# Expert matrices in runs of 8 KB: another order of the contraction rows in the expert layers of a two-layer hybrid model

## Chip, cores and metric

The kernel runs on one core of one Trainium2 chip. The metric is the device time of one execution in microseconds (us). Three runs of the kernel before are known: 1325.94, 1326.06 and 1327.15 us, with a median of 1326.06 us. The profiled execution took 1326.32 us; its instructions span 1324.5 us.

## The reference

Each of the two layers has a mixer (retention and RWKV-7), a cross-attention to a memory, and a mixture of experts; every one is followed by a layer norm. The change concerns the experts alone:

```python
# t: 256 tokens x 1024; 16 experts; combine[t, e] is nonzero for 2 experts of each token
for e in range(16):
    h = silu(t @ w_gate[e]) * (t @ w_up[e])      # w_gate, w_up: [1024, 512]
    y = y + combine[:, e:e+1] * (h @ w_down[e])  # w_down: [512, 1024]
```

All of it is float32. In both products a sum over the rows of a matrix (1024 or 512 of them) is taken, and the order of the rows in that sum is free.

## The kernel before

Weights come from HBM in pieces of 1 MB, all issued by SyncE (SP, line L150 in `fetch`). `piece` (L184) says which part of a matrix a piece is: with `(k p) c -> p k c` partition p gets the rows p, 128 + p, 256 + p and so on, so a partition's share of a piece lies in several separate places in HBM. A gate or up matrix is two pieces, each of four rows of 2 KB per partition; a down matrix is two pieces, each of two rows of 4 KB per partition. One layer's experts are 16 x 3 x 2 = 96 pieces. They go into a ring of buffers (tiles `raw`, `wh`, `x` and `A`; L1122 adds the last three for the expert stage). SP issues a piece as soon as its buffer has been read for the last time, so pieces are fetched far ahead of use.

`moe` (L1099) runs one layer of experts. L1107 to L1115 turn x around with TensorE and split it into two float32r parts (`rx`); `route` (L1021) computes from these which tokens go to which expert, in a long chain of small VectorE operations that begins with `big` (L1036). Beside it, L1117 to L1119 split x as it is, without turning it, into `xs[0]` and `xs[1]`: ScalarE copies x into the first (L135), and VectorE subtracts (L136) to get the rest. L1124 to L1127 put x itself into the accumulators `py` with eight multiplications by a unit matrix `identr`, of 512 columns each. `gather` (L1184), once for four experts, multiplies slices of 128 columns of `xs` by a one-hot matrix `oh`; out come the tokens of the four experts, already turned, as four tiles `xe`, each with two blocks of 128 model columns. The block index k there must mean the same model columns as the index k of the weight pieces.

L1132 to L1166 go over pairs of experts p. `expert_in` (L1231) does one gate or up product: two pieces, four multiplications each; the token block (`xe`, 64 columns) is stationary in TensorE and the weights stream through. Two multiplications for the upper and the lower half of the output rows lie side by side in the array; `halves` (L1242) adds the two halves with a ScalarE copy to `low` (L1246) and a VectorE addition (L1247). `expert_mid` (L1249) turns the activations of a pair, [128 tokens, 512], with four transposes of 128 columns each (`tr`, L131: the slice of the activation is loaded into TensorE as weights, and the unit matrix streams through); VectorE copies the result to `hT` (L1255). `expert_out` (L1258) is the down product. The PE rows of these products are `g<-raw,xe` and `g<-raw,hT` (or `wh`, `x`, `A` for `raw`), of the transposes `g<-cst,act`, of the unit-matrix products `y<-xs,identr`, of the gather `g<-oh,xs`. In these names the streamed operand stands before the loaded one. An instruction of the program in float32 can show as two rows: four multiplications of `expert_in` are eight matmuls in the trace.

A layer ends with `norm` (L269), the prefetch of two pieces for the next layer (L1173), a branch `tc.If(n > 0)` that all engines pass (L1175), and the layer norm. The body of the branch, `overflow` (L1289), is for an expert with more than 64 tokens. No instruction of it is in the trace. After the first layer's branch `memory` (L942) loads the memory `mem` again in four parts into `sg` (L951), turns them and starts the next layer's products.

Program order is not the order of an engine: a scheduler lays out each engine's instructions by their dependences when the program is built. One line of `moe` (L1139) forces an order, that the first expert's products stand behind the first one-hot.

Of the kernel before, what the change touches and what calls it, by code (L numbers as in the profile page):

```python
# [9 lines left out]
F32 = mybir.dt.float32  # L10
# [10 lines left out]
D = 1024  # L21
DK = D // 128
# [3 lines left out]
FE = 512  # L26
# [78 lines left out]
def flat(ap):  # L105

    n = len(ap.shape) - 1
    names = " ".join("abcdefg"[:n])
    return ap.rearrange(f"p {names} -> p ({names})") if n > 1 else ap
# [6 lines left out]
class Build:  # L116
# [66 lines left out]
    @staticmethod  # L183
    def piece(w, k0, nk, c0, n):  # L184
        return w.rearrange("(k p) c -> p k c", p=128)[:, k0:k0 + nk, c0:c0 + n], [128, nk, n]

    @staticmethod
    def finish(steps):
# [910 lines left out]
    def moe(self, l, x, mem):  # L1099
        tc, nc, a, c = self.tc, self.nc, self.a, self.c  # L1100
        wg, wu, wd = a["moe_w_gate"][l], a["moe_w_up"][l], a["moe_w_down"][l]
        py = [[self.pp.tile([128, 512], F32, name="y", tag="a", bufs=2) for _ in range(2)]]
        with ExitStack() as ctx:
            mo = ctx.enter_context(tc.tile_pool(name="moe", bufs=1))
            with tc.tile_pool(name="route", bufs=1) as rp:
                rx = []
                for k in range(0, DK, 2):  # L1107
                    ps = self.pp.tile([128, 2, 2, 128], F32, name="g", tag="b", bufs=4)
                    for j in range(2):
                        for tb in range(2):  # L1110
                            self.tr(ps[:, j, tb, :], x[:, tb, (k + j) * 128:(k + j + 1) * 128])
                    if k % 4 == 0:
                        t = self.wpool.tile([128, 2, 2, 2, 256], F32R, name="rx", tag="wh", bufs=self.nhi)
                    rx.append([t[:, k // 2 % 2, i] for i in range(2)])
                    self.split(flat(ps), flat(rx[-1][0]), flat(rx[-1][1]))  # L1115
                rank, cws, cover, flag = self.route(rx, rp, mo, self.small)
            xs = [self.xt.tile([128, 2, D], F32R, name=f"xs{i}", tag=f"xT{i}") for i in range(2)]  # L1117
            for tb in range(2):
                self.split(x[:, tb, :], xs[0][:, tb, :], xs[1][:, tb, :])  # L1119
            if l + 1 < self.layers:  # L1120
                self.spill_values(l + 1, mem, 0)
            self.ring = self.ring + [(self.wpool, "wh", self.nhi)] * self.nhi + [(self.xp, "x", 1)] + ([(self.aux, "A", 2)] * 2 if l + 1 < self.layers else [])  # L1122
            py.append([self.pp.tile([128, 512], F32, name="y", tag="c", bufs=2) for _ in range(2)])
            for tb in range(2):  # L1124
                for jc in range(2):
                    for i in range(2):
                        self.mm(py[tb][jc], self.identr, xs[i][:, tb, jc * 512:jc * 512 + 512], i == 0, False)  # L1127
            lists, acts, ys = {}, {}, {}
            step = self.gather(mo, 0, xs, rank, cws, lists)
            self.finish(step)  # L1130

            for p in range(NP + 2):  # L1132
                if p < NP:
                    if p % 2 == 0 and p < NP - 2:
                        step = self.gather(mo, p // 2 + 1, xs, rank, cws, lists)
                    xe = lists[p // 2][0]
                    act = mo.tile([128, 512], F32, name="act", bufs=2)
                    for o in range(2):
                        with self.behind(self.onehot) if p == 0 and o == 0 and NM > 0 else ExitStack():  # L1139
                            ps = self.expert_in(wg[2 * p + o], [t[:, :, 2 * (p % 2) + o] for t in xe])  # L1140
                        self.halves(mo, ps, act, o)
                        next(step, None)
                    nc.scalar.activation(act, act, AF.Silu)
                    acts[p] = act
                if 1 <= p <= NP:
                    hT = self.expert_mid(mo, acts.pop(p - 1))
                if p < NP:
                    if p >= 2:
                        self.combine(p - 2, ys.pop(p - 2), lists[(p - 2) // 2][1][:, p % 2], py)
                    us = self.aux.tile([128, 512], F32, name="us", tag="sg", bufs=3)  # L1150
                    for o in range(2):
                        ps = self.expert_in(wu[2 * p + o], [t[:, :, 2 * (p % 2) + o] for t in xe])
                        self.halves(mo, ps, us, o)
                        next(step, None)
                    nc.vector.tensor_mul(out=act, in0=act, in1=us)
                    if p % 2:
                        self.finish(step)
                if 1 <= p <= NP:
                    y = [self.aux.tile([128, 512], F32, name="y", tag="sg", bufs=3) for _ in range(2)]
                    for o in range(2):  # L1160
                        self.expert_out(mo, wd[2 * p - 2 + o], hT, y, o)
                        if p == NP and o == 0:
                            self.combine(p - 2, ys.pop(p - 2), lists[(p - 2) // 2][1][:, p % 2], py)
                    ys[p - 1] = self.weighed(mo, y, lists[(p - 1) // 2][2][:, (p - 1) % 2:(p - 1) % 2 + 1])
                if p == NP + 1:
                    self.combine(p - 2, ys.pop(p - 2), lists[(p - 2) // 2][1][:, p % 2], py)  # L1166
        self.extra.close()
        self.ring = [r for r in self.ring if r[1] == "raw2"]
        gb = self.norm(a["ln3_g"][l], a["ln3_b"][l])
        self.ring = [(self.wpool, "raw", self.nraw)] * self.nraw  # L1170
        if l + 1 < self.layers:
            w = a["xa_wkv"][l + 1]
            self.prefetch([self.piece(w, hf * 4, 4, D + 512, 512) for hf in range(2)])  # L1173
        n = nc.values_load(flag[0:1, 0:1], min_val=0, max_val=2 * S)
        with tc.If(n > 0):  # L1175
            self.overflow(l, xs, py, cover)
        x = self.xp.tile([128, 2, D], F32, name="x")

        self.layer_norm(lambda tb, j: py[tb][j], gb, x, LN_EPS / ALPHA ** 2)
        self.tail.close()  # L1180
        self.tap("ln3", x)
        return x
# [48 lines left out]
    def expert_in(self, w, xe):  # L1231

        ps = self.pp.tile([128, 512], F32, name="g", tag="b", bufs=4)
        for hf in range(2):
            raw = self.take(*self.piece(w, hf * 4, 4, 0, FE))
            for k in range(0, 4, 2):
                t = xe[hf * 2 + k // 2]
                for j in range(2):
                    self.mm(ps[j * 64:j * 64 + 64, :], t[:, j], raw[:, k + j, :], hf == 0 and k == 0, hf == 1 and k == 2)
        return ps  # L1240
# [8 lines left out]
    def expert_mid(self, mo, g):  # L1249

        ps = self.pp.tile([128, 4, 128], F32, name="g", tag="b", bufs=4)
        for f in range(4):
            self.tr(ps[:, f, :], g[:, f * 128:f * 128 + 128])
        hT = mo.tile([128, 4, 128], F32, name="hT", bufs=1)
        self.nc.vector.tensor_copy(out=flat(hT), in_=flat(ps))  # L1255
        return hT

    def expert_out(self, mo, wd, hT, y, o):  # L1258

        pd = [self.pp.tile([128, 512], F32, name="g", tag="b", bufs=4) for _ in range(2)]  # L1260
        for hf in range(2):
            raw = self.take(*self.piece(wd, hf * 2, 2, 0, D))
            for jc in range(2):
                for j in range(2):
                    self.mm(pd[jc][j * 64:j * 64 + 64, :], hT[:, hf * 2 + j, o * 64:o * 64 + 64], raw[:, j, jc * 512:jc * 512 + 512], hf == 0, hf == 1)
        for jc in range(2):
            self.halves(mo, pd[jc], y[jc], o)
# [21 lines left out]
    def overflow(self, l, xs, py, cover):  # L1289

        tc, nc, a = self.tc, self.nc, self.a
        pp = self.pp
        with tc.tile_pool(name="ov", bufs=1) as op:
            x = op.tile([128, 2, D], F32, name="ox")
            nc.vector.tensor_add(out=flat(x), in0=flat(xs[0]).bitcast(F32), in1=flat(xs[1]).bitcast(F32))
            xT = op.tile([128, DK, 256], F32, name="oxT")
            for k in range(0, DK, 2):
                ps = pp.tile([128, 2, 2, 128], F32, name="otp", tag="b", bufs=4)
# [4 lines left out]
            with tc.For_i(0, NE, 1) as e:  # L1303
                wd = op.tile([128, 4, D], F32, name="owd")
# [4 lines left out]
                for fh in range(2):  # L1309
                    w = []  # L1310
# [54 lines left out]
```

## Time and profile before

| | |
|---|---|
| runs | 1325.94, 1326.06, 1327.15 us |
| profiled execution | 1326.32 us, its span 1324.5 us |
| TensorE busy (PE) | 1225.4 us, 93% of the span |
| TensorE weight loads (PEld) | 856.1 us, beside PE |
| VectorE (DVE) | 759.1 us, 57% |
| ScalarE (ACT) | 494.9 us, 37% |
| GpSimd (POOL) | 73.0 us, 6% |
| DMA | 331.10 MB, mean 250 GB/s |

A line of the profile names line, engine, operation, what is written and what is read, the shape, and the count; behind the bar stand the busy time, the mean time of one in ns, and the idle time of the engine before it with what ended that. The timeline gives start, duration and the same names, equal neighbours merged. The expert stage of the first layer lies between 463 and 685 us, that of the second between 1085 and 1312 us.

### The profile page before, as it was taken

The page shows a single profiled execution, that of the slowest core. Times are in us where ns is not written, and L with a number is a line of the kernel's source. Part 1 is how long each engine was busy: PE and PEld are TensorE (multiplying, and loading weights), DVE is VectorE, ACT ScalarE, POOL GpSimd, SP SyncE. Part 2 cuts the span into 40 slices and gives each one's busy share as a digit, 9 for nine tenths or more (in the row PEclk, how much of TensorE's full clock was granted, in tenths as well). Part 3 has the DMA queues.
Part 4 walks back from the last instruction along what each step waited for, and adds up shares of the span by engine and source line. Part 5 has one row for each costly group of instructions (what it writes and reads, how often), then busy time and mean ns, then how long its engine had stood idle before and what let it go on. Part 6 is the DMA issues. An engine that isn't in the chain of part 4 may idle for free. (4 is left out here: it accounts for less than half of the span.)

```text
span 1324.5 us, 20023 instructions
## 1 busy us (share of the span) xinstructions
PE 1225.4 (93%) x7952; PEld 856.1 (65%) x7952; DVE 759.1 (57%) x1518; ACT 494.9 (37%) x785; POOL 73.0 (6%) x125
## 2 busy tenths in 40 slices
PE   7998998998999999999969998989979969999995
PEld 7886687796888844333329976877959854434331
DVE  6588677487557523333366787865775562333335
ACT  4556333253544322322235663332534312232222
POOL 0012221000000000000000103210000000000000
PEclk9999989999999999999989999999999979999997
DMA  9745132198834899999997452231888349999994
GB/s 318 263 148 180 50 97 76 33 323 290 276 127 175 304 398 402 398 397 402 399 341 228 159 179 72 85 96 48 302 291 312 120 166 349 402 396 401 401 396 194
DMA packets 189843, 331.10 MB, mean 250 GB/s; under 512 B 23152, under 2 KB 80880, under 8 KB 188720
## 3 DMA queue, kind: packets, MB, share of 16 engines
q1 hardware_dynamic: 187728, 324.51, 68.2%
q10 hardware_dynamic: 1728, 3.15, 0.7%
q0 software_dynamic: 288, 2.10, 0.4%
q8 instruction: 66, 1.08, 0.3%
q14 instruction: 33, 0.27, 0.1%
HBM read 321.86 MB, written 7.87 MB: 249 GB/s over the span
## 5 line engine op out<-in xcount | busy, mean ns | idle before, releaser
L136 DVE TENSOR_TENSOR wh<-raw,wh 128x1024 fp32r<-128x1024 f32 (+1 forms) x204 | 232.7, 1143 | 111.0 <-ACT wh L135 109.5
L135 ACT CAST wh<-raw 128x1024 fp32r<-128x1024 f32 (+1 forms) x204 | 199.8, 981 | 155.0 <-PE acc L127 138.5
L127 PE MATMUL acc<-xT,wh 128*128 128x256 f32 x1824 | 247.7, 289 | 2.7 <-DVE xT L136 1.6
L127 PEld LDWEIGHTS acc<-xT,wh 128*128 128x128 f32 x1824 | 225.9, 190 | 11.2 <-DVE xT L136 1.9
L1246 ACT COPY low<-g 64x512 f32<-64x512 f32 x128 | 74.2, 580 | 289.4 <-PE g L127 263.5
L127 PE MATMUL g<-raw,xe 128*64 128x512 f32 x688 | 157.7, 598 | 4.5 <-DVE hT L1255 3.4
L127 PE MATMUL acc<-wh,xT 128*128 128x512 f32 x384 | 101.9, 408 | 3.0 <-DVE vg L557 3.0
L127 PEld LDWEIGHTS g<-raw,xe 128*64 128x64 f32 x688 | 46.0, 136 | 90.7 <-issue 79.9
L1247 DVE TENSOR_TENSOR y<-g,low 64x512 f32<-64x512 f32 x64 | 44.1, 689 | 77.0 <-ACT low L1246 75.8
L127 PE MATMUL g<-raw,hT 128*64 128x512 f32 x352 | 81.4, 596 | 5.2 <-DVE hT L1255 2.6
L127 PEld LDWEIGHTS acc<-wh,xT 128*128 128x128 f32 x384 | 70.1, 188 | 21.5 <-DVE vg L557 3.8
L1247 DVE TENSOR_TENSOR us<-g,low 64x512 f32<-64x512 f32 x32 | 22.0, 689 | 94.4 <-ACT low L1246 94.3
L1247 DVE TENSOR_TENSOR act<-g,low 64x512 f32<-64x512 f32 x32 | 22.0, 689 | 75.2 <-ACT low L1246 75.1
L127 PEld LDWEIGHTS g<-raw,hT 128*64 128x64 f32 x352 | 26.1, 137 | 54.6 <-issue 41.7
L127 PE MATMUL acc<-wh,memT 128*128 128x512 f32 x192 | 51.0, 417 | 0.0
L127 PE MATMUL acc<-memT,wh 128*128 128x256 f32 x384 | 46.5, 282 | 1.6 <-DVE wh L136 1.2
L127 PEld LDWEIGHTS acc<-memT,wh 128*128 128x128 f32 x384 | 45.7, 188 | 2.6 <-DVE wh L136 1.7
L127 PE MATMUL acc<-wh,oT 128*128 128x512 f32 x192 | 45.6, 394 | 1.0 <-DVE x L406 0.8
L127 PE MATMUL acc<-wh,mT 128*128 128x512 f32 x192 | 45.7, 397 | 0.7 <-DVE xr L406 0.7
L127 PE MATMUL acc<-ys,wh 128*128 128x256 f32 x384 | 45.1, 279 | 0.0
L127 PEld LDWEIGHTS acc<-ys,wh 128*128 128x128 f32 x384 | 45.0, 188 | 0.0
L127 PEld LDWEIGHTS g<-oh,xs 128*128 128x128 f32 x256 | 33.4, 196 | 17.1 <-issue 11.2
(310 smaller groups left out, 1700.6 us busy)
## 6 DMA issues: line engine op xcount, KB each, us to landing
raw<-in_w_in_dram SPq DMA_DIRECT2D x46, 1024.0 KB, 5.1
raw<-in_moe_w_down_dram SPq DMA_DIRECT2D x44, 1024.0 KB, 14.9
raw<-in_moe_w_gate_dram SPq DMA_DIRECT2D x43, 1024.0 KB, 13.9
raw<-in_moe_w_up_dram SPq DMA_DIRECT2D x43, 1024.0 KB, 13.8
raw<-in_xa_wkv_dram SPq DMA_DIRECT2D x16, 1024.0 KB, 10.2
wh<-in_moe_w_up_dram SPq DMA_DIRECT2D x15, 1024.0 KB, 14.2
A<-in_moe_w_down_dram SPq DMA_DIRECT2D x10, 1024.0 KB, 13.6
A<-in_moe_w_gate_dram SPq DMA_DIRECT2D x9, 1024.0 KB, 13.7
```

The lines of the kernel that those rows point to most:

```text
L127: self.nc.tensor.matmul(out, lhsT, rhs, start=start, stop=stop, skip_group_check=True)
L135: self.nc.scalar.copy(out=hi, in_=src)
L136: (eng or self.nc.vector).tensor_sub(out=lo, in0=src, in1=hi)
L1246: self.nc.scalar.copy(out=low[h], in_=ps[x])
L1247: self.nc.vector.tensor_add(out=out[h], in0=ps[h], in1=low[h])
```

## The change

The rows of the expert matrices are dealt to the partitions in another way: with `(p k) c -> p k c` partition p gets neighbouring rows, 8p to 8p + 7 of a gate or up matrix and 4p to 4p + 3 of a down matrix. A piece, half of these rows, is then one run of 8 KB in HBM per partition. Three things follow. `xs` is written with its columns in the matching order: the split reads x in steps of eight elements and writes neighbouring places, so that the slices that `gather` takes stay as they were. The products with the unit matrix must put x back into its own order, so their streamed operand is read across `xs` in steps of 128 elements. And the transposes of `expert_mid` take each fourth column of the activation. `overflow` gets two additions in the other order for its one.

```diff
+    def together(w, hf):
+        n = w.shape[0] // 128
+        return w.rearrange("(p k) c -> p k c", k=n)[:, hf * (n // 2):hf * (n // 2) + n // 2, :], [128, n // 2, w.shape[1]]
...
             for tb in range(2):
-                self.split(x[:, tb, :], xs[0][:, tb, :], xs[1][:, tb, :])
+                self.split(*(t[:, tb, :].rearrange(r, k=DK) for t, r in ((x, "q (p k) -> q k p"), (xs[0], "q (k p) -> q k p"), (xs[1], "q (k p) -> q k p"))))
...
-                        self.mm(py[tb][jc], self.identr, xs[i][:, tb, jc * 512:jc * 512 + 512], i == 0, False)
+                        self.mm(py[tb][jc], self.identr, xs[i][:, tb, :].rearrange("q (k p) -> q p k", k=DK)[:, jc * 64:jc * 64 + 64, :], i == 0, False)
...
-            raw = self.take(*self.piece(w, hf * 4, 4, 0, FE))
+            raw = self.take(*self.together(w, hf))
...
-            self.tr(ps[:, f, :], g[:, f * 128:f * 128 + 128])
+            self.tr(ps[:, f, :], g[:, f:FE:4])
...
-            raw = self.take(*self.piece(wd, hf * 2, 2, 0, D))
+            raw = self.take(*self.together(wd, hf))
```

## Rows read from the trace of the kernel before

**Rows 1.** The head of the page: span, and busy time of the engines.

```profile
span 1324.5 us, 20023 instructions
PE 1225.4 (93%) x7952; PEld 856.1 (65%) x7952; DVE 759.1 (57%) x1518; ACT 494.9 (37%) x785; POOL 73.0 (6%) x125
```

**Rows 2.** Stretches of 20 us, second layer: busy by engine, PEclk, DMA share, GB/s; sum.

```profile
1120.00:1140.00 20.00, 19.79 (x94) 7.15 (x96) 8.54 (x13) 7.31 (x12) 0.00 (x0) 1.00 1.04 398
...
sum 80.00, PE 77.94 PEld 29.08 DVE 33.02 ACT 26.19 POOL 0.00; mean PE 19.48 PEld 7.27 DVE 8.26 ACT 6.55 POOL 0.00
```

**Rows 3.** Waits in 470 to 685 us: total us, times, longest us.

```profile
PE g L127 <- DVE hT L1255: 3.4, 4, 1.3
...
PE g L127 <- DVE y L1247: 2.5, 5, 0.5
...
PE g L127 <- DMA raw<-in_moe_w_down_dram: 0.4, 1, 0.4
```

**Rows 4.** First layer, timeline of SP and PE: an early and a late piece.

```profile
501.23 4.71 SPq L150 DMA_DIRECT2D A<-in_moe_w_gate_dram  x1
...
539.88 1.51 PE L127 MATMUL g<-A,xe 128*64 128x512 f32 x6
...
649.40 11.82 SPq L150 DMA_DIRECT2D raw<-in_moe_w_down_dram  x6
...
664.23 1.94 PE L127 MATMUL g<-raw,hT 128*64 128x512 f32 x8 [0.38 <-DMA raw<-in_moe_w_down_dram]
```

**Rows 5.** DMA issues at 501.2 and 649.4 us, issue to landing in us.

```profile
A<-in_moe_w_gate_dram SPq DMA_DIRECT2D x1, 1024.0 KB, 16.0
...
raw<-in_moe_w_down_dram SPq DMA_DIRECT2D x1, 1024.0 KB, 14.7
```

**Rows 6.** DMA packets in 541 to 553 us, in 657 to 675 us; a transfer in 8 KB rows.

```profile
DMA packets 2323, 4.63 MB, mean 386 GB/s; under 512 B 67, under 2 KB 67, under 8 KB 2322
...
DMA packets 1932, 7.45 MB, mean 414 GB/s; under 512 B 116, under 2 KB 116, under 8 KB 1931
...
kT<-keys SPq DMA_DIRECT2D x2, 1024.0 KB, 4.8
```

**Rows 7.** Groups on DVE, shapes apart: L812 reads in steps of 16 elements, L814 doesn't.

```profile
L812 DVE TENSOR_TENSOR blkT<-blkO,blkM 64x225 f32<-64x225 f32 x4 | 2.1, 535 | 0.1
...
L814 DVE TENSOR_REDUCE blkO<-blkT 64x15 f32<-64x225 f32 x4 | 1.5, 379 | 0.1
...
L812 DVE TENSOR_TENSOR blkT<-blkO,blkM 64x1 f32<-64x1 f32 x4 | 0.6, 147 | 1.5 <-DMA blkM<-blkin 1.5
```

**Rows 8.** The split of x for the gather, shapes apart; second layer's timeline, DVE.

```profile
L136 DVE TENSOR_TENSOR xs<-x,xs 128x1024 fp32r<-128x1024 f32 x4 | 4.9, 1218 | 0.5 <-ACT xs L135 0.5
...
L135 ACT CAST xs<-x 128x1024 fp32r<-128x1024 f32 x4 | 4.2, 1046 | 15.4 <-DVE x L301 15.4
...
1072.26 2.48 DVE L136 TENSOR_TENSOR rx<-g,rx 128x512 fp32r<-128x512 f32 x4
```

**Rows 9.** PE timeline: unit-matrix products, first layer, then second layer up to the router.

```profile
441.98 0.87 PE L127 MATMUL y<-xs,identr 128*128 128x512 f32 x3
442.69 1.09 PE L127 MATMUL g<-rx,rw 128*32 128x256 f32 x8
...
1072.30 2.06 PE L127 MATMUL y<-xs,identr 128*128 128x512 f32 x4
1074.15 1.53 PE L127 MATMUL g<-rx,rw 128*32 128x256 f32 x9
...
1076.44 0.52 PE L127 MATMUL g<-rx,rw 128*32 128x256 f32 x3
```

**Rows 10.** Transposes of the activation: all weight loads as a group; one set, timeline.

```profile
L131 PEld LDWEIGHTS g<-cst,act 128*128 128x128 f32 x64 | 7.0, 141 | 8.4 <-issue 7.3 <-DVE y L1247 0.8
...
1230.30 0.42 PEld L131 LDWEIGHTS g<-cst,act 128*128 128x128 f32 x4 [0.81 <-issue]
```

**Rows 11.** The chain that ended last, 680 to 700 us: start, us, what.

```profile
684.68 2.74 DMA sg<-in_mem_dram
```

More of the change, by code (lines that the diff above doesn't have):

```diff
@@ L185, in piece @@
         return w.rearrange("(k p) c -> p k c", p=128)[:, k0:k0 + nk, c0:c0 + n], [128, nk, n]
+    @staticmethod
+    def together(w, hf):
+        n = w.shape[0] // 128
+        return w.rearrange("(p k) c -> p k c", k=n)[:, hf * (n // 2):hf * (n // 2) + n // 2, :], [128, n // 2, w.shape[1]]
     @staticmethod
@@ L1294, in overflow @@
             x = op.tile([128, 2, D], F32, name="ox")
-            nc.vector.tensor_add(out=flat(x), in0=flat(xs[0]).bitcast(F32), in1=flat(xs[1]).bitcast(F32))
+            for tb in range(2):
+                nc.vector.tensor_add(out=x[:, tb, :].rearrange("q (p k) -> q k p", k=DK), in0=xs[0][:, tb, :].bitcast(F32).rearrange("q (k p) -> q k p", k=DK),
+                                     in1=xs[1][:, tb, :].bitcast(F32).rearrange("q (k p) -> q k p", k=DK))
             xT = op.tile([128, DK, 256], F32, name="oxT")
```

## The prediction

> **What bounds the kernel now.** I began at the head of the page: TensorE is busy in 93% of the span, so time is won or lost mostly there [rows 1]. In the expert stage the windows show two resources that are full at once: in four stretches of 20 us PE is busy for 19.48 us of each on the mean at full clock, and the DMA engines move about 400 GB/s with a share at 1 [rows 2]. Shares don't say which of the two ends last, so I went on to the waits: in the first layer's expert stage PE waited 3.4 us for `hT`, 2.5 us for the additions of L1247, and 0.4 us for a weight piece [rows 3]. Then to single pieces. One is issued at 501.23 us, lands 16.0 us later, at 517.2 us, and is first used at 539.88 us: it lies ready for 22.6 us. A late one, issued at 649.40 us, lands 14.7 us later, at 664.1 us, and its product starts at 664.23 us, after a wait of 0.38 us [rows 4, 5]. So TensorE sets the pace nearly to the end of the stage; the DMA falls behind it, uses up the lead of 22.6 us, and the two meet in the last pieces only. What speeds up transfers can win the little that is waited for there; what lengthens TensorE's work counts in full.
>
> **The transfers.** Nothing is added to or taken from SP's or POOL's queue: 192 pieces of 1 MB stay 192, in the same order. The packets are fewer. A stretch with rows of 2 KB alone moved 386 GB/s, one with rows of 4 KB alone 414 GB/s [rows 6]: 1,048,576 bytes take 2.72 and 2.53 us. Per piece that is 512 and 256 packets over 16 engines, 32 and 16 on each, so 16 packets cost 0.18 us, or 11.4 ns each. With 8 KB there are 8 on each engine, and my estimate is 2.53 - 8 x 0.0114 = 2.44 us. An expert has four pieces of the first kind and two of the second: 15.94 us now, 14.64 us then, and 20.8 us less of transfers for a layer's 16 experts. The other bound: a whole transfer in 8 KB rows landed in 4.8 us and is not seen to beat the 4 KB rows [rows 6]; at their price the saving is 12 us. I take the first, since the two rates are long stretches and the other is one short transfer; it matters little, because these microseconds lie beside TensorE's work. On the path I count the wait of 0.4 us and, after the branch, the load of the memory: its first part takes 2.74 us on the chain [rows 11] right behind the last weights, and might come 0.4 us sooner. Together -0.8 us, with 0 and -1.5 us as bounds. What is late next when the pieces are early: the same waits for `hT` and L1247 as now.
>
> **The price of a long step.** Three edits read SBUF in steps of 8, 128 and 4 elements, where neighbours were read. Nearest in the trace is L812, whose first operand goes in steps of 16 elements: 225 elements take 535 ns and one takes 147 ns, so 1.73 ns for each. L814 has the same number of elements in the same number of rows, without a step: (379 - 147) / 224 = 1.04 ns [rows 7]. The long step costs 0.69 ns per element, in this row of VectorE. No row shows TensorE or ScalarE with one; for them it is bounded by nothing on one side and by one element per 1.73 ns on the other. A gain is excluded: the same elements are read, only farther apart. I take 1.73 ns for all three, as it is the only row there is and all three read the same memory.
>
> [...]
>
> **The split of x.** VectorE's share grows by 1024 x 0.69 = 0.7 us on top of 1.22 us, ScalarE's copy, with that price, by 0.7 us on top of 1.05 us [rows 8]; twice per layer. In the first layer both stand beside products of the memory that TensorE has in stock, so they cost nothing; without that cover it would be 1.4 us. In the second layer the first of them stands ahead of the four splits `rx` at 1072.26 us [rows 8], for which the router waits: 1.4 us later, in the chain with the next edit.
>
> **The unit-matrix products.** In the first layer three of them start 0.71 us before the next product, 0.24 us each [rows 9]. 512 elements at 1.73 ns are 0.89 us: 0.65 us more each. In the first layer eight stand in a gapless row of PE work: +5.2 us. In the second, four stand ahead of the router's products at 1072.30 us, two more between them, and two behind [rows 9]. There the rest of the first split is ready at about 1073.7 instead of 1072.3 us; two products that read it take until 1075.5 us, then come the router's products and two more of these, which now end at 1076.96 us, 2.81 us after 1074.15. After: 1075.5 + 2.81 + 2 x 0.65 = 1079.6 us, so +2.7 us with the split in it. The last two run while VectorE routes, at no cost. Bounds for both layers: 1.4 us (the split alone) and 7.9 us; I take 7.9.
>
> **The transposes.** 64 loads of 128 columns take 141 ns each now, and four of a set take 0.42 us [rows 10]. At 1.73 ns a column a load is 221 ns, so +0.08 us each, +0.32 us a set, +5.1 us for the 16 sets, since PE is full there. Bounds: 0, if the loads vanish beneath products before them, and 64 x (0.221 - 0.105) = 7.4 us, if nothing overlaps. I take 5.1. Behind a set wait VectorE's copy to `hT` and the down product.
>
> [...]
>
> **The rest.** `overflow` is not entered; its two additions cost nothing. The one-hot, the gather's products and the copies keep their shapes and steps.
>
> **Sum.** 1326.3 - 0.8 + 5.2 + 2.7 + 5.1 = 1338.5 us against the profiled execution, which stands 0.3 us above the median; 1338 us in terms of the median. With all upper bounds: 1326.3 + 7.9 + 7.4 = 1341.6 us.
>
> **Rivals.** (1) TensorE doesn't feel the step: then ScalarE and VectorE alone pay, 1.4 us in the second layer, against -0.8 us: 1327 us, no change. For it: its streams and loads have rows without steps only, and those take 0.24 us for 512 columns [rows 9], far quicker per element than VectorE, so its reading may work otherwise. Against: L812 [rows 7].
>
> (2) Faster: the weights bind more than the waits say. A wait for several things is put down to the last, and some of PE's idle time may be transfers in disguise. All of it is 20 - 19.48 = 0.52 us in 20 [rows 2], 5.8 us in a stage of some 225 us, 11.6 us for both. If TensorE doesn't feel the step and half of it goes, 5.8 + 0.8 - 1.4 = 5.2 us are won: 1321 us. It decides from 1.4 us of hidden waiting on. Against it: the 22.6 us for which an early piece lies ready [rows 4, 5].
>
> (3) Pieces in runs of 8 KB, one per 16 KB, move more slowly than now. No row has this pattern. As the lead is used up at the end of a stage [rows 4], each per cent of 16 x 15.94 = 255 us is then waited for in full: 5% would be 12.8 us a layer, 1364 us with the other terms. For it speaks nothing but that it isn't shown.
>
> That the change doesn't do what it says, and the runs stay short, I see no place for: in the new view the k index and the columns are neighbours.
>
> **How the numbers follow.** About 0.2%, 2.65 us, is what a measurement of this kernel can tell from no change. Forecast, TensorE pays for the step: 0.57; its own range goes from 1332 us, where streams pay little, to 1343 us. No change, rival 1: 0.25, 1324 to 1328.7 us. Faster, rival 2: 0.12. Above 1343 us, rival 3 or a new layout of the instructions that costs more: 0.06. So faster 0.12, same 0.25, slower 0.63. The range that leaves out about 2 in 10 reaches from the forecast down over rival 1 and over the upper bounds: 1324 to 1343 us.
>
> **What would show it.** Right: `y<-xs,identr` goes from 0.24 to about 0.9 us each, loads of `g<-cst,act` from 141 to about 220 ns, `xs` from 1.22 to 1.9 us; the packets of a layer's pieces fall from 64 x 512 + 32 x 256 = 40,960 to 96 x 128 = 12,288, with more GB/s while a piece moves, and DMA's share drops below 1 in the expert stage because SP waits for buffers; PE is busier there. Wrong: these rows keep their times (rival 1), or they do and the stage from the first product to the last `y<-yl` still shrinks by some microseconds (rival 2), or landing times grow while the GB/s falls (rival 3). A changed order of PE's instructions could cover any of these by a few microseconds.

## The result and the profile after

The changed kernel takes 1341.16 us (median of 20 runs, 1332.33 to 1354.07) beside 1332.0 us for the kernel before on the same chips (20 runs, 1323.58 to 1341.6). The ratio is 1.0082 with a 95% interval of [1.0055, 1.0108], so +10.9 us with [7.3, 14.4]; the two medians lie 9.2 us apart. The kernel is slower by under 1%, as forecast, and near the predicted size. Runs more than 1.5% above the fastest of their kernel are left out of the ratios, and of the estimate from clocks further down. How much of that size was for the reasons given is what the rest is about.

The head of the changed kernel's page, to be read beside [rows 1]:

```profile
span 1344.2 us, 20023 instructions
PE 1244.5 (93%) x7952; PEld 869.0 (65%) x7952; DVE 762.6 (57%) x1518; ACT 498.7 (37%) x785; POOL 72.7 (5%) x125
...
DMA packets 132499, 331.10 MB, mean 246 GB/s; under 512 B 23152, under 2 KB 80880, under 8 KB 106800
```

The instructions stand in the same order on PE, ACT and POOL, and on DVE but for the second addition in `overflow`, which isn't entered; SP issues the same pieces. So no difference between these two is an effect of the layout. Before, the page counts 189,843 packets; the difference of 57,344 is exactly the two layers' 2 x (40,960 - 12,288) of the prediction.

**The transfers did what they should.** The windows of the second expert stage, after (columns as in [rows 2]):

```profile
1140.00:1160.00 20.00, 20.00 (x98) 7.14 (x96) 7.68 (x11) 7.01 (x12) 0.00 (x0) 1.00 1.01 422
...
sum 80.00, PE 78.38 PEld 33.32 DVE 28.57 ACT 23.42 POOL 0.00; mean PE 19.59 PEld 8.33 DVE 7.14 ACT 5.85 POOL 0.00
```

422 GB/s in place of about 400: 2.48 us a piece, where the prediction estimated 2.44. PE is busy for 19.59 us of 20 here and for 19.50 in four windows spread over the stage, 19.48 before [rows 2]: that PE would be busier doesn't show. The late piece of [rows 4] in the changed kernel: its issue and its first product in the timeline (SP, PE), and its time to landing in the DMA view of 632.4 to 632.6 us:

```profile
632.50 0.33 SPq L150 DMA_DIRECT2D raw<-in_moe_w_down_dram  x1
...
665.17 1.89 PE L127 MATMUL g<-raw,hT 128*64 128x512 f32 x8
```

```profile
raw<-in_moe_w_down_dram SPq DMA_DIRECT2D x1, 1024.0 KB, 19.7
```

It lands at 652.2 us and lies ready for 13.0 us; before, its product started 0.1 us after the landing [rows 4, 5]. The waits of SP in 470 to 685 us show who limits the transfers now (total, times, longest; `g` and `y` are products of PE):

```profile
SPq L150 <- PE g L127: 115.2, 69, 4.9
...
SPq L150 <- DMA raw<-in_moe_w_down_dram: 15.9, 10, 2.1
```

SP still waits for PE to give buffers back, and in part for earlier pieces; DMA's share is 1.01 in the window above, where the prediction expected it below 1; over the first stage it is 0.97 (1.04 before), with 391 to 430 GB/s in the first 38 of 40 equal slices, so nearly all of a stage is still one row of transfers. PE's waits in the same stretch:

```profile
PE g L127 <- DVE y L1254: 2.5, 5, 0.5
...
PE g L127 <- DVE hT L1262: 2.1, 3, 0.8
PE g L127 <- ACT low L1253: 1.3, 1, 1.3
```

The 0.4 us on a piece [rows 3] is gone, and nothing else: the longest wait for `hT`, 1.3 us, is only named after `low` now (it stands at the same product, with 1.32 us in both timelines). That is all that 13 us of lead won.

**The prices of the steps.** Groups of the changed kernel, shapes apart, on DVE, ACT, PE and PEld (beside [rows 8] and [rows 10]):

```profile
L136 DVE TENSOR_TENSOR xs<-x,xs 128x1024 fp32r<-128x1024 f32 x4 | 8.3, 2083 | 1.8 <-ACT xs L135 1.8
...
L135 ACT CAST xs<-x 128x1024 fp32r<-128x1024 f32 x4 | 8.7, 2180 | 15.4 <-DVE x L307 15.4
...
L127 PE MATMUL y<-xs,identr 128*128 128x512 f32 x16 | 9.9, 704 | 1.3 <-DVE xs L136 1.3
...
L131 PEld LDWEIGHTS g<-cst,act 128*128 128x128 f32 x64 | 9.1, 208 | 8.3 <-issue 8.1
```

Per element that is 0.84 ns more on VectorE (865 ns over 1024), 1.11 on ScalarE (1134 over 1024), 0.52 in a load (67 over 128). A product's own 704 ns overlap the next, which starts 0.49 us later in the timeline below, so PE's price is read from starts. The timeline of PE in the first layer, after:

```profile
438.20 1.91 PE L131 MATMUL g<-cst,x 128*128 128x128 f32 x16
...
441.03 1.67 PE L127 MATMUL y<-xs,identr 128*128 128x512 f32 x3
442.50 1.14 PE L127 MATMUL g<-rx,rw 128*32 128x256 f32 x8
...
464.24 1.94 PE L127 MATMUL g<-raw,xe 128*64 128x512 f32 x8
...
679.53 1.03 PE L127 MATMUL g<-raw,hT 128*64 128x512 f32 x4
```

Three products in 1.47 us are 0.49 us each, where 0.24 us stood [rows 9]: 0.25 us more, not 0.65.

**Where the 20 us between the two profiled executions lie** (spans of 1324.5 and 1344.2 us). Some 6.6 of them lie in the two expert layers. Most of the rest, about 13.6 us, arises between 710 and 940 us, in the second layer's mixer, which the change doesn't touch; there the windows of the changed kernel show PEclk (the column after POOL's) at 0.65 and 0.58, where the kernel before has 1.00 in both:

```profile
900.00:920.00 20.00, 20.00 (x126) 14.56 (x125) 7.57 (x27) 1.90 (x5) 0.00 (x0) 0.65 0.21 79
920.00:940.00 20.00, 20.00 (x101) 15.27 (x101) 5.47 (x19) 4.06 (x8) 0.00 (x0) 0.58 0.00 1
```

TensorE was busy all through these 40 us; in windows of 1 us PEclk is 1.00 up to 906 us, 0.50 from 907 to 936 us and 1.00 again from 937 us on. The kernel before scatters by as much from run to run: its spans went from 1321.6 us at a mean clock of 0.975 to 1340.3 us at 0.962. So a whole time can't be read to a few microseconds from one execution, and I compared stretches. For each layer two are used: **route**, from the first row `g<-cst,x` (x is turned) to the first product with `xe`, and **experts**, from there to the end of the last product with `hT`; PEclk is 1.00 in every experts stretch, and in the first route of the kernel before and of the changed one; in the second route it is lower in both, 0.72 before and 0.68 after, so differences there hold a part that is the clock's (in the second route of the kernel before, sixteen products of the gather take 3.49 us at a PEclk of 0.55 and sixteen of the same shape 2.16 us at 1.00). In the first layer, after: 464.24 - 438.20 = 26.04 us, and 679.53 + 1.03 - 464.24 = 216.32 us. The kernel before has 23.92 and 216.34 us there, and 23.26 and 214.90 us in the second layer. All experiments in one table, as differences from these in us, and the whole time's ratio beside them:

| kernel | route 1 | experts 1 | route 2 | experts 2 | sum | ratio, 95% interval |
|---|---|---|---|---|---|---|
| the change | +2.1 | 0.0 | +3.9 | +0.6 | +6.6 | 1.0082 [1.0055, 1.0108] |
| runs alone | 0.0 | -0.6 | -0.1 | 0.0 | -0.7 | 0.998 [0.994, 1.0021] |
| steps alone | +2.1 | 0.0 | +3.6 | +0.6 | +6.3 | 1.0018 [0.998, 1.0056] |
| down alone | 0.0 | 0.0 | 0.0 | +0.6 | +0.6 | 1.001 [0.9971, 1.0048] |
| gate and up alone | +2.1 | -0.6 | +3.5 | 0.0 | +5.0 | 1.0063 [1.0022, 1.0103] |
| unit products without a step | 0.0 | 0.0 | +2.9 | +0.6 | +3.5 | 1.0027 [0.9989, 1.0064] |
| down, step of 2 | 0.0 | -0.1 | -0.1 | +0.6 | +0.4 | 0.9999 [0.9963, 1.0035] |
| down, VectorE writes the step | 0.0 | +0.3 | 0.0 | +1.0 | +1.4 | 1.002 [0.9986, 1.0054] |
| gather reads the step of 8 | +3.7 | +11.5 | +3.5 | +12.1 | +30.8 | 1.0253 [1.0204, 1.0303] |
| gather reads a step of 4 | +3.5 | +10.8 | +3.4 | +11.4 | +29.1 | 1.0184 [1.011, 1.0259] |
| fewer buffers, before | 0.0 | +16.1 | +0.2 | +9.8 | +26.0 | 1.018 [1.0129, 1.023] |
| fewer buffers, the change | +2.1 | +3.1 | +3.5 | +1.4 | +10.1 | 1.0065 [1.0029, 1.0101] |

The order of the instructions on every engine is that of the kernel before in all of them but the last two, which share another.

### The profile page after: what moved, and what is told of

Same layout as the page of the kernel before. It is cut to its first block, busy times and chain, and to the rows that moved or that the text cites. A ratio compares the mean times of both kernels' runs of the same rounds, so it can differ in the third digit from the quotient of the medians.

```text
span 1344.2 us, 20023 instructions
## 1 busy us (share of the span) xinstructions
PE 1244.5 (93%) x7952; PEld 869.0 (65%) x7952; DVE 762.6 (57%) x1518; ACT 498.7 (37%) x785; POOL 72.7 (5%) x125
## 5 line engine op out<-in xcount | busy, mean ns | idle before, releaser
L127 PE MATMUL acc<-xT,wh 128*128 128x256 f32 x1824 | 255.8, 295 | 3.1 <-DVE xT L136 2.0
L127 PEld LDWEIGHTS acc<-xT,wh 128*128 128x128 f32 x1824 | 232.7, 195 | 12.6 <-DVE xT L136 2.2
```

Of the source, the lines that this page charges most:

```text
L127: self.nc.tensor.matmul(out, lhsT, rhs, start=start, stop=stop, skip_group_check=True)
```

## The experiments

**The theory**: all of the loss comes from reads with a step, in TensorE's row of work and in the chain of the router; the faster transfers are covered by the lead of the ring. **The rival**: the 8 KB runs themselves disturb something. Two kernels take the change apart into transfers and reads.

Runs alone (rows and tokens don't match in it, so the sums are over other pairs of numbers; the work is the same):

```diff
 # the kernel before
-            raw = self.take(*self.piece(w, hf * 4, 4, 0, FE))
+            raw = self.take(*self.together(w, hf))
...
-            raw = self.take(*self.piece(wd, hf * 2, 2, 0, D))
+            raw = self.take(*self.together(wd, hf))
```

> The kernel before with the 8 KB runs alone: no step is read anywhere (rows and tokens are paired wrongly, the amount of work is the same). Steps theory (all of the loss comes from the three reads with a step, early pieces are worth next to nothing): -0.5 us, ratio 0.9996, between 0.998 and 1.001; packets fall to about 132,500. Transfer theory (the 8 KB runs themselves disturb something, so that the 4 us of the loss that the stages around the steps don't show are theirs): +4 us, ratio 1.003. Theory of rival 2 (the weights bind by more than the waits say): -5 us, ratio 0.996.

Measured: ratio 0.998 with an interval that holds the forecast, and -0.7 us in the stretches, nearly all of it at the end of the first expert stage, where the one wait on a piece stood. The rival's +4 us isn't in these stretches, and neither is the gain of rival 2 of the prediction (weights bind by more than the waits say); the whole time alone would exclude the first (1.003) but not the second (0.996). This profiled execution also came out 12 us long in the second layer's mixer, without any step in it: its PEclk is 0.92 in 700 to 940 us, as the changed kernel's, and 0.99 in the kernel before.

Steps alone, the complement (again rows and tokens don't match):

```diff
 # the changed kernel
-            raw = self.take(*self.together(w, hf))
+            raw = self.take(*self.piece(w, hf * 4, 4, 0, FE))
...
-            raw = self.take(*self.together(wd, hf))
+            raw = self.take(*self.piece(wd, hf * 2, 2, 0, D))
```

> The changed kernel with the old pieces: the three reads with a step stay, the transfers are those of before (rows and tokens are paired wrongly, the amount of work is the same). Steps theory: at least the loss of the whole change, +11 us, ratio 1.008, and not under 1.006; if transfers and steps meet, a little more, since each lost microsecond is paid and nothing is given back. Transfer theory: +7 us, ratio 1.005, what the stages around the steps show.

Measured: +6.3 us in the stretches, with the changed kernel's 2.1 and 3.6 us in the routes, but a ratio of only 1.0018, under the 1.006 that I asked for. The steps carry the loss that the stretches show; the whole +11 us, which I had put down to them, this run doesn't show. Runs and steps add up to 5.6 of the 6.6 us. The first expert stage tells why not to all: with the old transfers it loses nothing, though its transposes are slower, and its timeline has no wait any more where [rows 4] show 0.38 us (the product starts behind the one before it). The stage began 2.1 us later and its transposes are slower; that this gave the late pieces the time that the 8 KB runs give is my reading, and by it the same 0.6 us can be won once only.

The change in halves. Down alone has the strided loads of the transposes, gate and up alone the split and the unit-matrix products:

```diff
 # the kernel before: down alone
-            self.tr(ps[:, f, :], g[:, f * 128:f * 128 + 128])
+            self.tr(ps[:, f, :], g[:, f:FE:4])
...
-            raw = self.take(*self.piece(wd, hf * 2, 2, 0, D))
+            raw = self.take(*self.together(wd, hf))
```

> The 8 KB runs for the down matrices alone, with the transposes' loads in steps of four; gate, up, the split of x and the unit-matrix products as before. By the prediction's price (0.32 us a set): +5.1 us, ratio 1.004. By the sets as the trace of the changed kernel shows them (0.66 us before, 0.75 us after, 16 sets): +1.4 us, ratio 1.001. If loads with a step are hidden: 1.000.

```diff
 # the changed kernel: gate and up alone
-            self.tr(ps[:, f, :], g[:, f:FE:4])
+            self.tr(ps[:, f, :], g[:, f * 128:f * 128 + 128])
...
-            raw = self.take(*self.together(wd, hf))
+            raw = self.take(*self.piece(wd, hf * 2, 2, 0, D))
```

> The 8 KB runs for gate and up alone, with the split of x and the unit-matrix products in steps; the transposes as before. By the trace of the changed kernel: about +2 us in the first layer and +3.9 us in the second up to the first expert, so +6 us, ratio 1.0045. If the transposes carry most of the loss: +2 us, ratio 1.0015. With the kernel of the down matrices alone it should add up to the whole change, 1.008, if nothing overlaps.

Measured: +0.6 and +5.0 us, 5.7 us together beside 6.6 for the whole, which also wins the first stage's 0.6 us only once. In the first layer down alone pays for its transposes with that 0.6 us. So eight sets cost 0.6 us a layer, 1.3 us in both: the +1.4 us read from the sets, not the predicted 5.1. A set in the timelines, of the kernel before and of the changed kernel:

```profile
1230.30 0.66 PE L131 MATMUL g<-cst,act 128*128 128x128 f32 x4
1231.74 7.09 PE L127 MATMUL g<-raw,xe 128*64 128x512 f32 x32 [0.78 <-DVE hT L1255]
```

```profile
1249.29 0.75 PE L131 MATMUL g<-cst,act 128*128 128x128 f32 x4
1250.82 5.37 PE L127 MATMUL g<-raw,xe 128*64 128x512 f32 x24 [0.78 <-DVE hT L1262]
```

From the first transpose to the product behind them it is 1.44 us, then 1.53: a set costs 0.09 us, though each of its four loads takes 67 ns longer, 0.27 us together. So most of a longer load lies beside products in these sets.

**Which step in the route.** In this kernel the unit-matrix products read neighbours again; the accumulators then start from x with its columns in another order:

```diff
-                        self.mm(py[tb][jc], self.identr, xs[i][:, tb, :].rearrange("q (k p) -> q p k", k=DK)[:, jc * 64:jc * 64 + 64, :], i == 0, False)
+                        self.mm(py[tb][jc], self.identr, xs[i][:, tb, jc * 512:jc * 512 + 512], i == 0, False)
```

> The changed kernel with the unit-matrix products reading xs in neighbours again (the accumulators then start from x with its columns in another order). Steps theory: each of the sixteen products takes about 0.24 us again, so the first layer from the first of them to the first product with xe takes 22.3 us as before instead of 24.4 us, and the second layer from the turning of x to the first product with xe keeps only what the split of x costs, about 25 us instead of 27.1 us (before: 23.3 us). In all about -4 us against the changed kernel; ratio to the kernel before 1.001 to 1.005. Prediction's price (0.65 us each): -6.5 us. If the split of x carries it, the second layer's stretch stays at 27 us.

Measured: the first layer's route loses nothing any more, so its +2.1 us were eight products at 0.25 us. The second layer's keeps 2.9 of 3.9 us; the forecast of 25 us there (+1.7) was too low. The timelines of PE and DVE, of the kernel before and then of this one (from the turn of x to the transposes of `big` 1077.46 - 1068.73 = 8.73 us and 1087.37 - 1076.20 = 11.17 us; the changed kernel needs 12.35 us):

```profile
1068.73 3.91 PE L131 MATMUL g<-cst,x 128*128 128x128 f32 x16 [7.03 <-DVE x L301]
...
1077.46 0.61 PE L127 MATMUL g<-cst,big 32*128 32x16 f32 x4
```

```profile
1071.11 1.23 DVE L136 TENSOR_TENSOR xs<-x,xs 128x1024 fp32r<-128x1024 f32 x1 [0.45 <-ACT xs L135]
```

```profile
1076.20 3.91 PE L131 MATMUL g<-cst,x 128*128 128x128 f32 x16 [7.03 <-DVE x L307]
1079.76 0.77 PE L127 MATMUL y<-xs,identr 128*128 128x512 f32 x1
1081.69 1.65 PE L127 MATMUL y<-xs,identr 128*128 128x512 f32 x3 [1.16 <-DVE xs L136]
1083.14 2.12 PE L127 MATMUL g<-rx,rw 128*32 128x256 f32 x9
...
1087.37 0.61 PE L127 MATMUL g<-cst,big 32*128 32x16 f32 x4
```

```profile
1079.62 2.01 DVE L136 TENSOR_TENSOR xs<-x,xs 128x1024 fp32r<-128x1024 f32 x1 [1.49 <-ACT xs L135]
1081.55 2.47 DVE L136 TENSOR_TENSOR rx<-g,rx 128x512 fp32r<-128x512 f32 x4
```

ScalarE's copy, 1.0 us longer, makes VectorE wait for 1.49 us in place of 0.45; then VectorE's own subtraction is 0.8 us longer, and the four `rx` and the products with `rw` stand behind both. The first product with `rw` starts 6.94 us after the turn of x, where it started after 5.42 us [rows 9], at a PEclk of 0.50 there and also here in 1081.6 to 1083.2 us: the split costs 1.5 us. The other 0.9 us up to the transposes of `big` are no step's. From there on no operand has one in this kernel, and yet it takes 4.23 us for 3.31. The windows of these products, before and here (columns as in [rows 2]):

```profile
1074.15:1077.46 3.31, 3.27 (x21) 2.37 (x19) 2.13 (x3) 0.06 (x1) 0.00 (x0) 0.90 1.05 402
```

```profile
1083.14:1087.37 4.23, 4.20 (x22) 2.94 (x20) 3.24 (x4) 0.36 (x1) 0.00 (x0) 0.68 0.75 240
```

TensorE has waited 1.2 us more before these products, and they run at a PEclk of 0.68 in place of 0.90. Behind the transposes of `big`, where no read differs either, this kernel loses 0.5 us more, and the changed kernel 0.3 us, at 0.66 and 0.65 in place of 0.77. The unit-matrix products with a step add 12.35 - 11.17 = 1.2 us. So of the changed kernel's +3.9 us about 1.5 are the split's, 1.2 the products' and 1.2 the granted clock's. The clock stood otherwise in each execution, so the last two may be off by some tenths; that the three other kernels with both steps have +3.5 and +3.6 us in this stretch suggests that the clock's part comes with them, but what brings it isn't shown.

**Does the distance matter, and is a step cheaper in a write?** A matrix can also be dealt within each half, which keeps 8 KB runs and halves the step:

```diff
 # the kernel before: down, step of 2
-            self.tr(ps[:, f, :], g[:, f * 128:f * 128 + 128])
+            self.tr(ps[:, f, :], g[:, f // 2 * 256 + f % 2:f // 2 * 256 + 256:2])
...
-            raw = self.take(*self.piece(wd, hf * 2, 2, 0, D))
+            raw = self.take(wd.rearrange("(h p k) c -> h p k c", p=128, k=2)[hf], [128, 2, D])
```

> 8 KB runs for the down matrices alone, dealt within each half of 256 rows, so that a partition takes two neighbouring rows and the transposes' loads read each second column in place of each fourth. If the price grows with the distance between elements: the loads take clearly less than 208 ns (141 ns without a step), and the expert stages lose 0 to 0.2 us each where the kernel of the down matrices in steps of four lost about 0.5 us; with the earlier pieces at the end -0.5 to -1 us in all, ratio 0.999. If any step costs the same: loads of 208 ns and the marks of that kernel, ratio 1.000.

```diff
 # down alone, with the natural transposes; VectorE writes act and us dealt
-        self.nc.vector.tensor_add(out=out[h], in0=ps[h], in1=low[h])
+        t = [out[h], ps[h], low[h]]
+        if deal:
+            t = [a.rearrange(r, f=4) for a, r in zip(t, ("q (f p) -> q p f", "q (p f) -> q p f", "q (p f) -> q p f"))]
+        self.nc.vector.tensor_add(out=t[0], in0=t[1], in1=t[2])
```

> 8 KB runs for the down matrices alone; the additions of the halves (VectorE) write the activations with their columns dealt, so that the transposes' loads read neighbours again. If a step in what VectorE writes is cheap: loads 141 ns, additions about 0.69 us as before, expert stages as in the kernel with runs alone, -0.5 to -1.5 us, ratio 0.999. If it costs what the split of x cost per element (0.85 ns): additions of 512 elements take 1.12 us; they end the wait of the transposes, four a pair and one of them in the chain, so up to 16 x 0.43 = +7 us, ratio 1.005.

The loads of the first, then the additions to `act` and the loads of the second, as groups:

```profile
L131 PEld LDWEIGHTS g<-cst,act 128*128 128x128 f32 x64 | 9.1, 207 | 8.3 <-issue 8.1
```

```profile
L1256 DVE TENSOR_TENSOR act<-g,low 64x512 f32<-64x512 f32 x32 | 34.4, 1075 | 72.4 <-ACT low L1252 72.3
...
L131 PEld LDWEIGHTS g<-cst,act 128*128 128x128 f32 x64 | 6.9, 141 | 8.9 <-issue 8.1 <-DVE act L1256 0.8
```

A step of two costs a load as much as a step of four (207 and 208 ns, 141 without), and the stretches agree: +0.6 us in the second expert stage in both. A step in a write is no cheaper: 0.69 becomes 1.07 us, 0.75 ns per element, and the loss is larger (+1.4 us) than with the step in the loads. Which wait carries it isn't shown: the row of loads names an addition for 0.8 us, as it did before [rows 10].

**Moving all of gate's and up's step to the gather.** x is split as before, the unit-matrix products read neighbours, and the 256 loads of `xs` carry the step, of eight or (dealt within halves) of four:

```diff
 # the changed kernel, with L1119 and L1127 as before; then the same at a step of 4
-                        self.mm(ps[:, j], xs[i][:, tb, k * 128:k * 128 + 128], oh[:, tb], j == 0 and tb == 0 and i == 0, tb == 1 and i == 1)
+                        self.mm(ps[:, j], xs[i][:, tb, k:D:DK], oh[:, tb], j == 0 and tb == 0 and i == 0, tb == 1 and i == 1)
...
+                        self.mm(ps[:, j], xs[i][:, tb, k // 4 * 512 + k % 4:k // 4 * 512 + 512:4], oh[:, tb], j == 0 and tb == 0 and i == 0, tb == 1 and i == 1)
...
-            raw = self.take(*self.together(w, hf))
+            raw = self.take(w.rearrange("(h p k) c -> h p k c", p=128, k=4)[hf], [128, 4, FE])
```

> The change with the step moved: x is split as before, the unit-matrix products read neighbours, and the 256 loads of the gather take each eighth column of xs. Steps theory: router stretch back at 23.3 us; the loads take about 67 ns more each, as those of the transposes did (141 to 208 ns), and as the transposes showed about a third of that reaches TensorE's spacing, so 256 x 0.022 = +5.6 us spread over both expert stages; ratio 1.002 to 1.006. If loads with a step hide beside products of 256 columns: ratio 0.998 to 1.001, a version without any loss. If all of it counts: 256 x 0.067 = +17 us, ratio 1.013.

> The kernel in which the gather's loads carry the step, with gate and up dealt within each half of 512 rows: a partition takes four neighbouring rows, still 8 KB in one run, and the 256 loads read each fourth column of xs in place of each eighth. If the price grows with the distance: between the 0.118 us of a product without a step and the 0.25 us at steps of eight, about 0.18 us, so the loss falls from +30 us to about +15 us, ratio 1.011. If a step of four already pays all: 0.25 us again, ratio 1.025.

The first misses all three of its forecasts, of which the highest was +17 us: +30.8 us. The second comes out as the second of its own, that a step of four already pays all: +29.1 us. Sixteen such products in the timelines of the kernel before, at a step of eight and at a step of four:

```profile
461.15 2.16 PE L127 MATMUL g<-oh,xs 128*128 128x256 f32 x16
463.24 0.65 PE L127 MATMUL g<-raw,xe 128*64 128x512 f32 x2
```

```profile
460.36 4.14 PE L127 MATMUL g<-oh,xs 128*128 128x256 f32 x16
464.43 3.65 PE L127 MATMUL g<-raw,xe 128*64 128x512 f32 x16
```

```profile
460.65 4.01 PE L127 MATMUL g<-oh,xs 128*128 128x256 f32 x16
464.59 3.65 PE L127 MATMUL g<-raw,xe 128*64 128x512 f32 x16
```

They go from 2.09 / 16 = 0.131 us to 0.254 and 0.246 us each, so 256 of them cost about 31 us. The loads as groups in 455 to 700 us, where the clock is full, without a step and with a step of eight:

```profile
L127 PEld LDWEIGHTS g<-oh,xs 128*128 128x128 f32 x128 | 16.2, 188 | 8.6 <-issue 6.0 <-DVE yl L1277 0.8 <-DVE ws L1224 0.8
```

```profile
L127 PEld LDWEIGHTS g<-oh,xs 128*128 128x128 f32 x128 | 31.9, 336 | 8.2 <-issue 5.7 <-DVE ws L1231 0.8 <-DVE y L1254 0.8
```

A load grows by 148 ns, and 0.123 us of it reaches the spacing of the products. I had carried over the transposes' price, but there four loads at a time stand behind long products, and here loads and short products alternate. That this is why so little is covered here is my reading; no run tests it by itself.

**When would the faster transfers pay?** Both kernels with less lead: the line that adds buffers for the expert pieces is left out of each.

```diff
-            self.ring = self.ring + [(self.wpool, "wh", self.nhi)] * self.nhi + [(self.xp, "x", 1)] + ([(self.aux, "A", 2)] * 2 if l + 1 < self.layers else [])
```

> The kernel before with fewer buffers for the expert pieces: the line that adds the wh, x and A buffers to the ring is left out. TensorE then starts the expert stage with about six pieces (about 14 us) less of a lead. Theory that transfers were worthless only because the ring's lead covers them: the late pieces, which now land 0 to 2 us before use, come late, and PE waits 10 to 14 us per layer on the weights; ratio 1.015 to 1.021. If the ring had more than it needs: ratio under 1.004.

> The changed kernel with the same fewer buffers. Its late pieces lie ready 12 to 14 us with the full ring, so the smaller ring costs it next to nothing: PE waits under 2 us per layer on weights, and the time stays at that of the changed kernel, ratio to the kernel before 1.005 to 1.009, that is 8 us or more below the kernel before with the same fewer buffers. If 8 KB runs don't move faster, both lose the same and the changed kernel stays 6 us or more above the other.

Measured: 1354.65 us for the kernel before and 1338.77 us for the changed kernel with the fewer buffers, 15.9 us apart the other way round; in the stretches +26.0 and +10.1 us against the kernel before. (The profiled execution of the first, 1369.2 us, stands above its median; its mean clock is 0.957, and its expert stages are at full clock.) PE's longest totals on weights in 470 to 705 us, with the fewer buffers, before and after:

```profile
PE g L127 <- DMA raw<-in_moe_w_down_dram: 5.6, 9, 0.7
PE g L127 <- DMA raw<-in_moe_w_up_dram: 5.5, 8, 0.9
...
PE g L127 <- DMA raw<-in_moe_w_gate_dram: 1.7, 2, 0.8
```

```profile
PE g L127 <- DMA raw<-in_moe_w_down_dram: 1.1, 2, 0.6
```

Here the change works as a change of transfers should: the waits on pieces fall from 12.8 to 1.1 us, and with them goes most of what the weights cost the stage. Both kernels come out as expected. Neither beats the kernel before with its full ring, and none of the twelve kernels is shown to; runs alone, which is no version of the computation, marks what there was to win: 0.7 us.

## Why the prediction was right or wrong

**The direction and its mechanism**: right. TensorE, not the weights, sets the pace; transfers became faster and landed 13 us early, for which PE got 0.6 us; the reads with a step cost more. Rival 1 (TensorE doesn't feel the step) falls by the rows of the products and the loads, rival 3 (slower pieces) by 422 GB/s, and rival 2 by the 0.7 us that the runs alone win in the stretches.

**The sizes**, term by term, predicted and measured:

- Transfers, -0.8 us: -0.7 us in the stretches with runs alone. Of the two parts the wait on the piece gave 0.6 us for 0.4; the load of `mem` after the branch lies outside the stretches and wasn't tested by itself; on the chain its first part takes 2.70 us in the changed kernel, 2.74 before [rows 11].
- The unit-matrix products, 0.65 us each: 0.25 us. This is one of the two steps of the prediction that failed: "512 elements at 1.73 ns" took VectorE's time per element for TensorE, where the difference to L814, 0.69 ns, was the part that the step costs; the row measured was 0.49 ns more per column. First layer +2.1 us in place of +5.2. The mechanism held and the size did not.
- The second layer's route, +2.7 us: +3.9. The split was near, 1.5 us for the predicted 1.4, though ScalarE pays 1.11 ns per element and not VectorE's price, which was used for it. The products came to 1.2 us for the predicted 1.3, but by other numbers: each costs less, and the last two, counted at nothing, stand ahead of the transposes of `big` (1.11 us from their start to those transposes, 0.67 us without the step). What the prediction had no term for is the granted clock: about 1.2 us go to products without a step that run at a lower one than before.
- The transposes, +5.1 us: 1.3 us. This is the other step that failed, and in us the larger miss. The price of a load was near (141 to 208 ns, +67; 80 predicted), but the sum took it as if a set's own row were all that PE does. 0.08 to 0.09 us a set reach the path, of 0.27 us of longer loads, so the lower bound of 0, with the loads beneath products before them, was nearer than the 5.1 us taken.

By these the expert layers lose 6.6 us, about half of the predicted 12.2. The runs' ratio says 10.9 us, and at least 7.3. What is more than 6.6 us must lie outside these stretches, and the profiled execution shows there only the lower granted clock. Of the twelve kernels in the table the changed one is the only one whose interval doesn't hold the sum of its stretches; steps alone, with the same reads, does. The mean granted clock of each run is on record and allows an estimate. A straight line through 76 runs of the kernel before in the experiments (time against mean clock, 1.1 us for each 0.001, with a scatter of 2.0 us) lies 4.1 us below the changed kernel's runs at their own clocks, 4.7 us below those of steps alone and 1.7 us above those of runs alone. The longer second route at 0.68 of full clock lowers the changed kernel's mean by about 0.0016 itself, which the line counts as 1.8 us; with that it is 5.9 us, near the stretches' 6.6. So what the ratio shows beyond the stretches goes with the clock: its mean is 0.963 in the changed kernel's runs, 0.968 in those of steps alone, 0.967 in those of the kernel before. Whether the lower clock was chance, or the change brings it about somewhere, isn't settled by these runs. That the median fell so near to 1338 us is therefore partly luck; and the kernel before, from whose 1326.06 us the prediction started, has a median of 1332.0 us over the 20 runs.

## What to carry to other kernels

Before giving a transfer a better shape, ask for how long its data lies ready: here, where an early piece lay ready for 22.6 us, the runs alone won 0.7 us in the stretches, and with fewer buffers the same change is worth 16 us. Price a step by the starts of neighbouring instructions in the same row, on the engine that sets the pace: here 64 longer loads that lay beside other products cost 1.3 us, and 256 that alternate with short products about 31 us. And where runs of one kernel scatter by more than the effect, compare stretches of equal clock from one mark to another, with one half of the change at a time.

## What the runs showed that was not expected

- In TensorE's loads the size of the step hardly matters in the steps that were run: loads of 128 columns take 141 ns without one, 207 ns at two, 208 ns at four elements; the gather's products 0.131 us without one, 0.246 us at four, 0.254 us at eight.
- The price per element differs by engine in these rows: 0.49 ns in TensorE's streamed operand, 0.52 in the transposes' loads, 0.84 on VectorE, 1.11 on ScalarE; a write with a step cost VectorE 0.75.
- A load in the gather paid about twice as much per column as one in the transposes: 148 ns over 128 columns, 1.16 ns. Both rows read 128x128 f32; `xs`, which the gather loads, is written as fp32r [rows 8]. Why isn't shown.
